# Decoder trunk on one core: merged columns written beside the last input tile, a second raw weight tile in the mixer, and its weights' low parts on GpSimd

## Chip, cores and metric

One NeuronCore of one Trainium2 chip runs the whole kernel in a single launch. The metric is the device time in microseconds. Two kernels are compared by the median of their runs.

## What is computed

The reference is one inference step of a decoder layer over 1024 prompt tokens and 8 sample tokens, in fp32. The stages are a half-step SwiGLU, a token mixer, cross-attention into 256 memory tokens and a second SwiGLU, each followed by a layer norm. The change lies in the mixer:

```python
def _mixer(h, S0, shift0, h0, buf0, P):
    proj = h @ P['w_in']                     # r, k, v, low-rank inputs, LRU input, GeLU gate, two merge gates
    ...
    S_new, y = _rwkv_scan(S0.astype(F32), rh, hd(decay), kh, vh, kk, hd(a))
    ...
    _, hs = lax.associative_scan(_lin_combine, (a_t, b_t), axis=1)
    lru_out = (hs * jax.nn.gelu(p_gelu.astype(F32))).astype(h.dtype)
    gates = jax.nn.sigmoid(p_gate).reshape(B, T, N_BRANCH, D_MODEL)
    merged = gates[:, :, 0] * rwkv_out + gates[:, :, 1] * lru_out
    out = merged @ P['w_mix_out']
    return out, S_new.astype(h.dtype), p_rwkv[:, -1], hs[:, -1].astype(h.dtype), new_buf
```

## The kernel before, in words

Activations lie with channels on the partitions: `HH` and `HL` hold the high and the low part (fp32 rounded for TensorE, and the rest) of 8 blocks of 128 channels by 1032 columns. Every product is three matmuls (`mm3`, L122 to L127): high by high, low by high, high by low. A weight block is made by `split_half` (L90): SP loads a raw tile of 128x512, ScalarE rounds it to `wh` (L99), VectorE subtracts to give `wl` (L100), and the raw tile is free again once both have read it.

The mixer's 16 heads are 8 pairs. After the low-rank inputs and the first two pairs' r, k, v, its long middle part has 16 units t (four pairs of pairs, `g`, by four pieces of 256 columns, `n`). A unit runs several generators side by side, recorded in 13 rounds (`rounds`, L49): `chain` of unit t-1 (the recurrence: each of four chunks has three products, with VectorE or ScalarE between them), `inverse` of unit t (31 dependent pairs of VectorE instructions, L548 and L930), `stage_unit` of t+1, `branches` (the LRU), `samples_b` or `samples_c` for the sample tokens, `post` of a finished chain, and a share of the filler. Each engine then runs its instructions in the order in which the recording and the framework's scheduler leave them; SP's queue carries every DMA of the kernel.

The filler is `gemms` (L658): 50 input tiles (`project`, L632), each 3 column groups of 344 by 8 blocks, then the 8 tiles of the output product over the first six blocks (`out_proj`, L1211). One step is two blocks, that is six matmuls; `FILL[t]` (L536) is the number of steps that unit t takes, and the last unit takes what is left. `load` is called behind each of a tile's first two groups and makes one half of the next tile's weight. There is one raw tile in this part (`S.rawseq`, L768) and four pairs of `wh`, `wl` (L769).

Merged blocks 0 to 5 go through DRAM (`MG`). The last input tile has to be done with a column group of `HH` before merged columns can take that group's place. In `out_proj`, at m == 0, each group waits for its six blocks: load `ev` from `MG`, ScalarE writes `HH`, VectorE writes `HL` (`direct`, L1031), one filler step for each block, and the group's matmuls follow:

```python
for m in range(KT):
    for c0, n in CH3:
        for k in range(kt) if m == 0 else ():
            ...
            e = tmp("ev", 344, 2)[:, :n]
            nc.sync.dma_start(out=e, in_=MG[k, :, c0:c0 + n])
            direct(k, c0, n, e)
            yield
        q = psg(n)
        yield from cols(W[m], c0, n, q, kt)
```

`ev` is also the tile through which every group's result leaves (L641, L1231). GpSimd's instructions in this part are the powers of `inv_norm` (L782, tiles `ivs` and `ivc`), a copy into `BN` (L875) and the powers for the sample tokens (L1126, L1197).

Of the kernel before, what the change touches and what calls it, by code (L numbers as in the profile page):

```python
# [10 lines left out]
F32 = mybir.dt.float32  # L11
# [8 lines left out]
NT = NP + NS  # L20
# [69 lines left out]
def split_half(S, src, nm="w", hp=None, view=lambda t: t, to=None):  # L90

    nc = S.nc
    raw = raw_tile(S)[:, :512]
    S.wdma.dma_start(out=view(raw), in_=src)
    if to is None:
        hp = hp or next(S.hlseq)
        to = [hp.tile([128, 512], F32R, tag=nm + x, name=nm + x) for x in "hl"]
    hi, lo = to
    nc.scalar.activation(out=hi, in_=raw, func=AF.Identity)  # L99
    nc.vector.tensor_tensor(out=lo, in0=raw, in1=hi.bitcast(F32), op=ALU.subtract)  # L100
    return hi, lo


# [371 lines left out]
def setup(ctx, tc, I):  # L475
    nc = tc.nc
    S = SimpleNamespace(tc=tc, nc=nc, pend=[])
    S.const = ctx.enter_context(tc.tile_pool(name="const", bufs=1))
    S.hp = ctx.enter_context(tc.tile_pool(name="hp", bufs=1))
    S.wraw = ctx.enter_context(tc.tile_pool(name="wraw", bufs=1))  # L480
    S.whl = ctx.enter_context(tc.tile_pool(name="whl", bufs=3))
    S.wdma = nc.sync
    S.dram = ctx.enter_context(tc.tile_pool(name="dram", bufs=1, space=bass.MemoryType.DRAM))
    S.ones_d = S.const.tile([128, 128], F32, name="ones_d")
    nc.vector.memset(S.ones_d, 1.0 / D)
    S.lng = S.const.tile([128, 4, KT], F32, name="lng")
    S.lnb = S.const.tile([128, 4, KT], F32, name="lnb")
    nc.sync.dma_start(out=S.lng, in_=I["ln_g"])
    nc.sync.dma_start(out=S.lnb, in_=I["ln_b"])
    S.mhalf = S.const.tile([128, 8], F32, name="mhalf")  # L490
    nc.vector.memset(S.mhalf, -0.5)
    S.ident = S.const.tile([128, 128], F32, name="ident")
    nc.sync.dma_start(out=S.ident, in_=I["cst"][:, 0:128])
    S.HH = S.hp.tile([128, KT, NT], F32R, name="HH")
    S.HL = S.hp.tile([128, KT, NT], F32R, name="HL")
    return S
# [36 lines left out]
DRAM = bass.MemoryType.DRAM  # L533
GR, GK, GV, GZ, GA, GL, GE, G1, G0, GG, GB, GM = range(12)

FILL = [42] * 11 + [37] * 5  # L536

LATE = ("ev", "ref", "dend", "scl", "sm", "wsb", "sf", "ysb", "gsq", "ivc", "lm")

# [1 line left out]
def mixer(octx, S, I, O, MG, HD, pre):  # L541
# [13 lines left out]
    with ExitStack() as ctx:  # L555
# [76 lines left out]
        def project(p, mt, gi, func, sc, w, cs, psg, pool, then=None):  # L632

            for c0, n in cs:
                q = psg(n)
                yield from cols(w, c0, n, q)
                if then and c0 < CH3[2][0]:
                    then()
                e = pool.tile([128, 344], F32, tag="ev", name="ev", bufs=2)[:, :n]
                ACT(e, q, func, scale=sc)  # L640
                nc.sync.dma_start(out=GD[p][:, gi, c0:c0 + n], in_=e)  # L641

# [15 lines left out]
        def gemms():  # L658
# [9 lines left out]
            W = [[] for _ in src]  # L668
            queue = itertools.chain(((W[j], x[:, 512 * i:512 * i + 512]) for j, x in enumerate(src) for i in range(2)))

            def load():
                for to, x in itertools.islice(queue, 1):
                    to.append(split_half(S, x))

            load()
            load()
            for j, (p, x, i) in enumerate(todo):
                yield from project(p, *x, W[j], CH3, psg, t1, load)
                ready.add((p, x[1]))
                if i in (2, 5):  # L680
                    ends(p, i == 2)
            ready.add("h")
            yield from out_proj(W[len(todo):], load)


        with ExitStack() as c2:
# [78 lines left out]
        actx = ctx.enter_context(ExitStack())  # L765
        stages = itertools.cycle([(st0, 1)] + [(actx.enter_context(tc.tile_pool(name="msa", bufs=4)), 2)] * 2)
        ta = actx.enter_context(tc.tile_pool(name="ma", bufs=1))
        S.rawseq = itertools.cycle([S.wraw])  # L768
        S.hlseq = itertools.cycle([S.whl] * 3 + [actx.enter_context(tc.tile_pool(name="mwhl", bufs=1))])  # L769
        pools.update(dict.fromkeys(("i", "m", "sc"), actx.enter_context(tc.tile_pool(name="mpa", bufs=1, space=PSUM))))  # L770

# [21 lines left out]
        def stage(U, i):  # L793
# [45 lines left out]
            yield  # L839
            pb = psm(w)  # L840
            nc.tensor.matmul(pb, ones1, s2, start=True, stop=True)
            bv = tmp("bv", 256, 2)
            TTo(bv, xv[:, 0:256], pb[:, 0:256], ALU.mult)
            nc.sync.dma_start(out=GD[p][:, GB, c0:c0 + 256], in_=bv)
            if n == 3:
# [124 lines left out]
        def branch(p, n, P):  # L970
# [36 lines left out]
            ACT(th, th, AF.Sqrt)  # L1007
            yield
            STT(gi, gi, 0.5, th, ALU.mult, ALU.mult)
            hs = tmp("lm", 264, 2)  # L1010
            nc.vector.tensor_tensor_scan(out=hs[:, 0:256], data0=gr[:, 0:256], data1=gi[:, 0:256],
                                         initial=0.0 if n == 0 else P.hl, op0=ALU.mult, op1=ALU.add)
            yield
# [194 lines left out]
            else:  # L1208
                direct(p, NP, NS, y)

        def out_proj(W, load):  # L1211

            kt = KT - 2
            for m in range(KT):
                for c0, n in CH3:
                    for k in range(kt) if m == 0 else ():
                        while not all(("mg", k, j) in ready for j in range(5) if c0 < (NT if j == 4 else 256 * j + 256) and
                                      256 * j < c0 + n):
                            yield

                        e = tmp("ev", 344, 2)[:, :n]
                        nc.sync.dma_start(out=e, in_=MG[k, :, c0:c0 + n])
                        direct(k, c0, n, e)
                        yield
                    q = psg(n)
                    yield from cols(W[m], c0, n, q, kt)
                    if c0 < CH3[2][0]:
                        load()
                    e = tmp("ev", 344, 2)[:, :n]
                    ACT(e, q, scale=1.0 / ALPHA)  # L1230
                    nc.sync.dma_start(out=FD[m, :, c0:c0 + n], in_=e)  # L1231

# [88 lines left out]
        actx.close()  # L1321
        S.norms = Norms(S, octx)
        more_weights(S, ctx, 2, 1)
        wp = ctx.enter_context(tc.tile_pool(name="wmix", bufs=4))
        fp = ctx.enter_context(tc.tile_pool(name="fmix", bufs=2))
        w = [[split_half(S, I["w_mix"][4 * i:4 * i + 4, :, 128 * k:128 * k + 128].rearrange("m p c -> p m c"), hp=wp,
# [383 lines left out]
```

## Time and profile before

| | before |
|---|---|
| median of 3 runs | 3221.41 us (3218.6 to 3223.76) |
| the profiled execution, its own time | 3223.72 us |
| its span from first to last instruction | 3221.9 us |
| mean granted TensorE clock | 0.964 |
| TensorE busy (PE) | 3029.4 us, 94% of the span |
| weight loads (PEld) | 2855.4 us, 89% |
| VectorE (DVE) busy | 2199.8 us, 68% |
| ScalarE (ACT) busy | 1433.5 us, 44% |
| GpSimd (POOL) busy | 560.8 us, 17% |

A busy share is an average over stages. A granted clock of 1 stands for 2.4 GHz and 0.5 for 1.2 GHz; a stretch in which both occurred shows a value between. Matmuls overlap, so the time of one in a dense run is the distance between two starts and not its own length. Line numbers are those of the kernel before.

### The profile page before, as it was taken

The page shows a single profiled execution, that of the slowest core. Times are in us where ns is not written, and L with a number is a line of the kernel's source. Part 1 is how long each engine was busy: PE and PEld are TensorE (multiplying, and loading weights), DVE is VectorE, ACT ScalarE, POOL GpSimd, SP SyncE. Part 2 cuts the span into 40 slices and gives each one's busy share as a digit, 9 for nine tenths or more (in the row PEclk, how much of TensorE's full clock was granted, in tenths as well). Part 3 has the DMA queues.
Part 4 walks back from the last instruction along what each step waited for, and adds up shares of the span by engine and source line. Part 5 has one row for each costly group of instructions (what it writes and reads, how often), then busy time and mean ns, then how long its engine had stood idle before and what let it go on. Part 6 is the DMA issues. An engine that isn't in the chain of part 4 may idle for free. (4 is left out here: it accounts for less than half of the span.)

```text
span 3221.9 us, 63123 instructions
## 1 busy us (share of the span) xinstructions
PE 3029.4 (94%) x23324; PEld 2855.4 (89%) x23324; DVE 2199.8 (68%) x5895; ACT 1433.5 (44%) x3192; POOL 560.8 (17%) x526
## 2 busy tenths in 40 slices
PE   8999999999999999998999888889898999999997
PEld 8999999999888888887888767688887999999997
DVE  7666665574357788777777777676677666666556
ACT  5333352125555565555555554464235433334112
POOL 2222200132000101010110100261005322220111
PEclk9999999999999999999999969799999999999998
DMA  4222253314544455445445544664433222225321
GB/s 140 80 79 80 80 162 106 106 54 145 192 117 127 135 142 147 118 135 147 141 126 140 144 140 115 200 186 133 148 121 116 79 80 80 80 80 157 107 86 53
DMA packets 381445, 386.72 MB, mean 120 GB/s; under 512 B 144048, under 2 KB 282320, under 8 KB 381136
## 3 DMA queue, kind: packets, MB, share of 16 engines
q1 hardware_dynamic: 381136, 382.69, 39.8%
q8 instruction: 183, 3.00, 0.4%
q14 instruction: 126, 1.03, 0.1%
HBM read 277.54 MB, written 105.23 MB: 119 GB/s over the span
## 5 line engine op out<-in xcount | busy, mean ns | idle before, releaser
L125 PE MATMUL ps<-HH,wh 128*128 128x258 f32 (+1 forms) x2384 | 718.3, 302 | 17.0 <-ACT HH L508 7.9
L126 PE MATMUL ps<-HL,wh 128*128 128x258 f32 (+1 forms) x2384 | 716.6, 301 | 0.0
L127 PE MATMUL ps<-HH,wl 128*128 128x258 f32 (+1 forms) x2384 | 715.7, 300 | 0.0
L125 PE MATMUL g<-HH,wh 128*128 128x344 f32 (+2 forms) x1840 | 625.0, 340 | 31.5 <-ACT wh L99 20.3
L127 PE MATMUL g<-HH,wl 128*128 128x344 f32 (+2 forms) x1840 | 598.9, 327 | 6.5 <-DVE wl L100 6.5
L126 PE MATMUL g<-HL,wh 128*128 128x344 f32 (+2 forms) x1840 | 602.0, 328 | 1.8 <-DVE HL L548 1.4
L125 PEld LDWEIGHTS ps<-HH,wh 128*128 128x128 f32 x2384 | 451.4, 189 | 19.2 <-ACT HH L508 7.9
L126 PEld LDWEIGHTS ps<-HL,wh 128*128 128x128 f32 x2384 | 450.9, 189 | 0.4 <-DVE HL L509 0.3
L127 PEld LDWEIGHTS ps<-HH,wl 128*128 128x128 f32 x2384 | 450.3, 189 | 0.0
L125 PEld LDWEIGHTS g<-HH,wh 128*128 128x128 f32 x1840 | 359.8, 196 | 50.3 <-ACT wh L99 22.6
L127 PEld LDWEIGHTS g<-HH,wl 128*128 128x128 f32 x1840 | 359.3, 196 | 12.2 <-DVE wl L100 8.0
L126 PEld LDWEIGHTS g<-HL,wh 128*128 128x128 f32 x1840 | 360.2, 196 | 9.3 <-DVE HL L548 3.4
L228 ACT ACTIVATE wh<-raw 128x512 fp32r<-128x512 f32 x280 | 176.4, 631 | 321.9 <-PE ps L126 264.8
L334 POOL TENSOR_TENSOR raw<-raw 128x512 f32<-128x512 f32 x160 | 214.1, 1338 | 566.2 <-DVE wl L229 351.3
L229 DVE TENSOR_TENSOR wl<-raw,wh 128x512 fp32r<-128x512 f32 x280 | 202.2, 723 | 138.9 <-ACT wh L228 132.0
L100 DVE TENSOR_TENSOR wl<-raw,wh 128x512 fp32r<-128x512 f32 x302 | 217.4, 726 | 109.9 <-ACT wh L99 104.8
L99 ACT ACTIVATE wh<-raw 128x512 fp32r<-128x512 f32 x302 | 185.5, 626 | 235.0 <-PE ps L126 78.0
L442 DVE SCALAR_TENSOR_TENSOR acc<-ps,acc 128x344 f32<-128x344 f32 x336 | 168.8, 512 | 144.2 <-PE ps L127 143.5
L548 DVE TENSOR_TENSOR pr<-tq,iv 128x2 f32<-128x2 f32 (+30 forms) x496 | 160.3, 323 | 2.9
L553 ACT ACTIVATE ev<-g 128x344 f32<-128x344 f32 x192 | 87.3, 455 | 127.9 <-PE g L127 97.5
L930 DVE TENSOR_REDUCE tq<-pr 128x1 f32<-128x2 f32 (+30 forms) x496 | 121.6, 245 | 2.8
L374 ACT ACTIVATE g<-g 128x258 f32<-128x258 f32 x160 | 67.1, 419 | 113.2 <-DVE g L333 113.2
(410 smaller groups left out, 6363.6 us busy)
## 6 DMA issues: line engine op xcount, KB each, us to landing
raw<-in_wi_dram SPq DMA_DIRECT2D x176, 256.0 KB
raw<-in_w_in_dram SPq DMA_DIRECT2D x116, 256.0 KB
GD<-ev SPq DMA_DIRECT2D x168, 172.0 KB
raw<-in_wo_dram SPq DMA_DIRECT2D x104, 256.0 KB
raw<-HID SPq DMA_DIRECT2D x88, 258.0 KB
HID<-g SPq DMA_DIRECT2D x80, 258.0 KB
tg<-GD SPq DMA_DIRECT2D x32, 512.0 KB
wt<-T SPq DMA_DIRECT2D x160, 64.0 KB
```

The costliest lines, as they stand in the source:

```text
L99: nc.scalar.activation(out=hi, in_=raw, func=AF.Identity)
L100: nc.vector.tensor_tensor(out=lo, in0=raw, in1=hi.bitcast(F32), op=ALU.subtract)
L125: nc.tensor.matmul(ps, wh, xh, start=first, stop=False)
L126: nc.tensor.matmul(ps, wh, xl, start=False, stop=False)
L127: nc.tensor.matmul(ps, wl, xh, start=False, stop=last)
L228: nc.scalar.activation(out=hi, in_=x, func=AF.Identity)
L229: nc.vector.tensor_tensor(out=lo, in0=x, in1=hi.bitcast(F32), op=ALU.subtract)
L334: pool_tt = lambda o, a, b, op: nc.gpsimd.tensor_tensor(out=o, in0=a, in1=b, op=op)
L442: nc.vector.scalar_tensor_tensor(out=a, in0=q, scalar=0.5 / ALPHA, in1=a, op0=ALU.mult, op1=ALU.add)
L548: TTo = lambda o, a, b, op: nc.vector.tensor_tensor(out=o, in0=a, in1=b, op=op)
L553: ACT = lambda o, a, f=AF.Identity, **kw: nc.scalar.activation(out=o, in_=a, func=f, **kw)
L930: nc.vector.tensor_reduce(out=tq[:, 0:m, i], in_=pv, axis=mybir.AxisListType.X, op=ALU.add)
```

## The change

Four things change in the mixer's middle part.

1. The merged columns of a group are no longer loaded and split at the head of `out_proj`. A generator `merged` for each group starts when the last input tile's matmuls of that group are recorded, and moves by two blocks at every following step of that tile. The last group's merges stay in `out_proj`, three steps instead of six.
2. The raw weight tile gets a second buffer (`mraw`), and `ev` a third. For their space `bv` and `lm` go from two buffers to one.
3. `FILL` goes from 37 to 34 steps in units 11 to 13 and to 40 in units 14 and 15.
4. `wl` of the weights made in this part, 116 of them, is subtracted by GpSimd in place of VectorE. Behind the units VectorE does it again.

```diff
-    nc.vector.tensor_tensor(out=lo, in0=raw, in1=hi.bitcast(F32), op=ALU.subtract)
+    S.low.tensor_tensor(out=lo, in0=raw, in1=hi.bitcast(F32), op=ALU.subtract)
...
-FILL = [42] * 11 + [37] * 5
+FILL = [42] * 11 + [34] * 3 + [40] * 2
...
-                if then and c0 < CH3[2][0]:
-                    then()
-                e = pool.tile([128, 344], F32, tag="ev", name="ev", bufs=2)[:, :n]
+                if then:
+                    then(c0, n)
+                e = pool.tile([128, 344], F32, tag="ev", name="ev", bufs=3 if then else 2)[:, :n]
...
-            for j, (p, x, i) in enumerate(todo):
+            for j, (p, x, i) in enumerate(todo[:-1]):
                 yield from project(p, *x, W[j], CH3, psg, t1, load)
...
-            ready.add("h")
-            yield from out_proj(W[len(todo):], load)
+            p, x, i = todo[-1]
+            merges = []
+            def then(c0, n):
+                load(c0, n)
+                merges.append(merged(c0, n))
+            for _ in project(p, *x, W[len(todo) - 1], CH3, psg, t1, then):
+                for m in merges:
+                    next(m, 0)
+                yield
+            ready.update(((p, x[1]), "h"))
+            yield from out_proj(W[len(todo):], load, merges)
...
-        S.rawseq = itertools.cycle([S.wraw])
+        S.rawseq = itertools.cycle([S.wraw, actx.enter_context(tc.tile_pool(name="mraw", bufs=1))])
+        S.low = nc.gpsimd
...
-            bv = tmp("bv", 256, 2)
+            bv = tmp("bv", 256)
...
-            hs = tmp("lm", 264, 2)
+            hs = tmp("lm", 264)
...
+        def merged(c0, n):
+            for k in range(KT - 2):
+                while not all(("mg", k, j) in ready for j in range(5) if c0 < (NT if j == 4 else 256 * j + 256) and
+                              256 * j < c0 + n):
+                    yield
+                e = tmp("ev", 344, 3)[:, :n]
+                nc.sync.dma_start(out=e, in_=MG[k, :, c0:c0 + n])
+                direct(k, c0, n, e)
+                if k % 2:
+                    yield
...
-                for c0, n in CH3:
-                    for k in range(kt) if m == 0 else ():
...
+                for j, (c0, n) in enumerate(CH3):
+                    if m == 0:
+                        yield from merges[j]
...
+        S.low = nc.vector
```

SP's queue in unit 13, where the merges begin. `GD7<-ev` is the result of one of the last input tile's column groups on its way out, `ev<-MG` the load of one merged block, `raw` a half of an output weight, and the rest belongs to the units. Before:

```order
L641 DMA GD7_8811<-ev_23177 128x344
L1222 DMA ev_23180<-MG_81 128x344
L1222 DMA ev_23184<-MG_81 128x344
L1185 DMA e0_25225<-GD7_8811 128x8
L1222 DMA ev_23188<-MG_81 128x344
L1060 DMA MG_81<-ysb_22842 128x256
L1043 DMA tg_23346<-GD6_8810 128x4x256
L1222 DMA ev_23221<-MG_81 128x344
L844 DMA GD7_8811<-bv_23205 128x256
L1222 DMA ev_23225<-MG_81 128x344
```

Now:

```order
L643 DMA GD7_8811<-ev_23118 128x344
L1233 DMA ev_23128<-MG_81 128x344
L1233 DMA ev_23132<-MG_81 128x344
L94 DMA raw_23400<-in_w_mix_dram 128x512
L1233 DMA ev_23142<-MG_81 128x344
L94 DMA raw_23483<-in_w_mix_dram 128x512
L1200 DMA e0_25210<-GD6_8810 128x8
L1233 DMA ev_23146<-MG_81 128x344
L1233 DMA ev_23156<-MG_81 128x344
L1075 DMA MG_81<-ysb_22789 128x256
L643 DMA GD7_8811<-ev_23205 128x344
```

Before, the row at the top is the tile's third group and no group's result follows among the merges; now it is the first, the second (last row shown, five rows left out ahead of it) leaves after the first group's merges, and two halves of output weights are loaded among them.

GpSimd's queue in the same kind of unit, some units earlier: `ivs` and `ivc` are the powers that a stage and a finished chain wait for, `BN` the copy in a stage. Before:

```order
L875 COPY BN_19192<-BN_19192 64x4x64
L782 TENSOR_TENSOR ivc_19327<-ivc_19327,mhalf_75 128x4
L1197 TENSOR_TENSOR w8_19292<-w8_19292,mhalf_75 128x8
L782 TENSOR_TENSOR ivs_19499<-ivs_19499,mhalf_75 128x4
L875 COPY BN_19617<-BN_19617 64x4x64
L782 TENSOR_TENSOR ivc_19888<-ivc_19888,mhalf_75 128x4
```

Now:

```order
L100 TENSOR_TENSOR wl_19385<-raw_19382,wh_19384 128x512
L1212 TENSOR_TENSOR w8_19295<-w8_19295,mhalf_75 128x8
L100 TENSOR_TENSOR wl_19541<-raw_19538,wh_19540 128x512
L100 TENSOR_TENSOR wl_19630<-raw_19627,wh_19629 128x512
L797 TENSOR_TENSOR ivs_19502<-ivs_19502,mhalf_75 128x4
L890 COPY BN_19620<-BN_19620 64x4x64
L100 TENSOR_TENSOR wl_19787<-raw_19784,wh_19786 128x512
L100 TENSOR_TENSOR wl_19876<-raw_19873,wh_19875 128x512
L797 TENSOR_TENSOR ivc_19891<-ivc_19891,mhalf_75 128x4
```

One or two low parts now stand ahead of nearly every power and copy.

TensorE's program tells how the filler is spread. Between the ends of two units' inverses it holds this many filler matmuls:

| unit | 7 | 8 | 9 | 10 | 11 | 12 | 13 | 14 | 15 |
|---|---|---|---|---|---|---|---|---|---|
| before | 252 | 228 | 276 | 252 | 231 | 221 | 166 | 168 | 246 |
| now | 252 | 252 | 252 | 252 | 212 | 212 | 194 | 216 | 198 |

The table counts rows of the program. In the same program the chain's twelve products (three for each of four chunks) are spread unevenly at the end: in unit 13, now, the last nine stand with 24 filler matmuls among them and the rest of the filler behind, where before the first nine had 60 among them and the last three came 72 later; in unit 14, now, eleven stand with 18 among them, where before they were spread over 150.

## Rows read from the trace of the kernel before

**Rows 1.** The page, busy time of each engine over the span, with its share and its instructions.

```profile
PE 3029.4 (94%) x23324; PEld 2855.4 (89%) x23324; DVE 2199.8 (68%) x5895; ACT 1433.5 (44%) x3192; POOL 560.8 (17%) x526
```

**Rows 2.** Windows from the start of one unit's inverse (the memset of its tile `iv`) to the next, units 7 to 15 in order; the last ends where the filler ends. Columns: the stretch and its length in us, busy time of PE, PEld, DVE, ACT and POOL with instructions, granted clock, share of the DMA engines, GB/s.

```profile
1389.40:1462.60 73.20, 68.89 (x589) 60.47 (x588) 58.16 (x189) 41.95 (x91) 6.37 (x6) 0.98 0.53 142
1462.60:1540.80 78.20, 70.17 (x563) 62.30 (x562) 58.15 (x197) 42.02 (x94) 5.57 (x6) 0.91 0.52 146
1540.80:1607.20 66.40, 64.15 (x568) 56.79 (x567) 50.76 (x183) 40.34 (x96) 9.27 (x8) 1.00 0.48 139
1607.20:1676.20 69.00, 66.16 (x577) 59.24 (x576) 52.41 (x194) 39.15 (x94) 9.20 (x8) 0.98 0.46 126
1676.20:1748.50 72.30, 70.11 (x596) 60.42 (x595) 56.33 (x185) 40.51 (x89) 5.62 (x6) 0.98 0.55 147
1748.50:1827.70 79.20, 70.45 (x566) 59.57 (x566) 58.61 (x202) 41.12 (x92) 5.17 (x6) 0.89 0.51 135
1827.70:1898.90 71.20, 58.71 (x434) 46.11 (x433) 59.93 (x210) 43.44 (x106) 9.89 (x9) 0.76 0.44 124
1898.90:1972.30 73.40, 66.23 (x471) 56.06 (x470) 49.44 (x173) 42.95 (x100) 7.68 (x6) 0.86 0.46 134
1972.30:2041.20 68.90, 52.10 (x385) 44.99 (x384) 51.29 (x175) 27.76 (x53) 2.20 (x2) 0.85 0.50 130
```

**Rows 3.** Timeline of SP in units 13 and 15: start, duration (with what merged rows span), queue, line, DMA.

```profile
1878.81 9.42 SPq L1222 DMA_DIRECT2D ev<-MG  x2
...
2021.85 0.55 SPq L1174 DMA_DIRECT2D out_srwkv_dram<-ws  x1
2022.49 0.38 SPq L94 DMA_DIRECT2D raw<-in_w_mix_dram  x1
```

**Rows 4.** Windows of 5 us in unit 13, columns as in rows 2.

```profile
1865.00:1870.00 5.00, 4.01 (x23) 3.10 (x24) 4.96 (x21) 3.27 (x9) 0.78 (x1) 0.50 0.30 59
1885.00:1890.00 5.00, 4.21 (x36) 2.98 (x35) 4.01 (x15) 2.09 (x6) 1.12 (x1) 0.50 0.20 61
```

**Rows 5.** Timeline of PE in unit 15, two filler matmuls at the high clock and two at the low one: start, duration, line, operation.

```profile
2012.33 0.32 PE L127 MATMUL g<-HH,wl 128*128 128x344 f32 x1
2012.49 0.32 PE L125 MATMUL g<-HH,wh 128*128 128x344 f32 x1
...
2028.39 0.49 PE L127 MATMUL g<-HH,wl 128*128 128x344 f32 x1
2028.67 0.49 PE L125 MATMUL g<-HH,wh 128*128 128x344 f32 x1
```

**Rows 6.** Who PE waited for in the units, 880 to 2040 us: total, times, longest.

```profile
PE g L125 <- ACT wh L99: 19.0, 7, 6.7
PE m L788 <- ACT s L553: 16.2, 11, 5.0
...
PE g L127 <- DVE wl L100: 6.5, 3, 3.3
```

**Rows 7.** Timeline of PE, stalls on weights; in brackets the idle time ahead of the instruction and what ended it.

```profile
1184.61 0.66 PE L125 MATMUL g<-HH,wh 128*128 128x344 f32 x1 [3.55 <-ACT wh L99]
...
1471.40 0.66 PE L125 MATMUL g<-HH,wh 128*128 128x344 f32 x1 [4.18 <-ACT wh L99]
...
2003.17 0.66 PE L127 MATMUL g<-HH,wl 128*128 128x344 f32 x1 [2.75 <-DVE wl L100]
...
2026.64 0.66 PE L125 MATMUL g<-HH,wh 128*128 128x344 f32 x1 [6.66 <-ACT wh L99]
```

**Rows 8.** Timeline of ACT around two of these stalls.

```profile
1183.32 0.42 ACT L553 ACTIVATE cs<-cs 128x256 f32<-128x256 f32 x1 [0.66 <-DVE tq L930]
...
1183.95 0.61 ACT L99 ACTIVATE wh<-raw 128x512 fp32r<-128x512 f32 x1
...
2003.35 0.46 ACT L553 ACTIVATE ev<-g 128x344 f32<-128x344 f32 x1 [4.42 <-DMA FD<-ev]
...
2025.96 0.63 ACT L99 ACTIVATE wh<-raw 128x512 fp32r<-128x512 f32 x1 [2.75 <-DMA raw<-in_w_mix_dram]
```

**Rows 9.** Who SP's queue waited for at the raw weight loads (L94) in the units: total, times, longest.

```profile
SPq L94 <- DVE tq L930: 36.9, 21, 5.3
...
SPq L94 <- DVE pr L548: 21.1, 17, 3.2
```

**Rows 10.** Groups by line in the units, 880 to 2040 us: VectorE's largest group (the products in the inverse), its low parts, and GpSimd's powers of the stages. Columns: count, busy time and mean ns of one, idle time ahead of them and what ended it.

```profile
L548 DVE TENSOR_TENSOR pr<-tq,iv 128x2 f32<-128x2 f32 (+30 forms) x496 | 160.3, 323 | 2.9
...
L100 DVE TENSOR_TENSOR wl<-raw,wh 128x512 fp32r<-128x512 f32 x110 | 75.4, 686 | 33.0 <-ACT wh L99 31.4 <-DMA R<-GD 0.8 <-PE sc L881 0.5
L782 POOL TENSOR_TENSOR ivs<-ivs,mhalf 128x4 f32<-128x4 f32 x31 | 33.4, 1076 | 273.3 <-DVE ivs L551 235.7 <-DVE iv L922 25.2 <-ACT QZ L553 12.0
```

**Rows 11.** By tile over the whole span: GpSimd's sums of raw weights in the SwiGLU stages, and VectorE's low parts of merged blocks; duration min/median/max in ns.

```profile
L334 POOL TENSOR_TENSOR raw<-raw x160: 1270/1296/2296, 34.9 to 2901.0; 128x512 f32<-128x512 f32 x160
L548 DVE TENSOR_TENSOR HL<-ev,HH x18: 498/510/519, 1857.9 to 1924.2; 128x344 fp32r<-128x344 f32 x18
```

**Rows 12.** Timeline of the first SwiGLU, GpSimd and VectorE side by side.

```profile
113.25 2.95 POOL L334 TENSOR_TENSOR raw<-raw 128x512 f32<-128x512 f32 x2 [7.90 <-DVE u L333]
...
114.16 0.42 DVE L333 TENSOR_TENSOR u<-u,ps 128x258 f32<-128x258 f32 x1 [0.54 <-PE ps L127]
...
114.97 1.78 DVE L229 TENSOR_TENSOR wl<-raw,wh 128x512 fp32r<-128x512 f32 x1
```

More of the change, by code (lines that the diff above doesn't have):

```diff
@@ L669, in gemms, with load @@
             queue = itertools.chain(((W[j], x[:, 512 * i:512 * i + 512]) for j, x in enumerate(src) for i in range(2)))
-            def load():
-                for to, x in itertools.islice(queue, 1):
+            def load(c0=0, n=0):
+                for to, x in itertools.islice(queue, c0 < CH3[2][0]):
                     to.append(split_half(S, x))
@@ L1209, in samples_c, with out_proj @@
                 direct(p, NP, NS, y)
-        def out_proj(W, load):
-            kt = KT - 2
-            for m in range(KT):
-                for c0, n in CH3:
-                    for k in range(kt) if m == 0 else ():
[L1217 to L1224, printed above, removed]
+        def merged(c0, n):
[8 more added lines that the diff above has]
+                    yield
+        def out_proj(W, load, merges):
+            for m in range(KT):
+                for j, (c0, n) in enumerate(CH3):
+                    if m == 0:
+                        yield from merges[j]
                     q = psg(n)
[L1226 to L1229, printed above, removed]
+                    yield from cols(W[m], c0, n, q, KT - 2)
+                    load(c0, n)
+                    e = tmp("ev", 344, 3)[:, :n]
                     ACT(e, q, scale=1.0 / ALPHA)
@@ L1323, in mixer @@
         more_weights(S, ctx, 2, 1)
+        S.low = nc.vector
         wp = ctx.enter_context(tc.tile_pool(name="wmix", bufs=4))
```

## Prediction

> **What bounds the kernel now.** I read the page's busy times first: PE is busy for 94% of the span, DVE for 68% [rows 1]. So TensorE's work is nearly the time, and what can be won is its idle time and the time that it spends at the lower of its two clocks. The second view is the windows by unit of the mixer's middle part [rows 2]. The reader is to compare units at the same place of their four: 13 with 9, 14 with 10, 15 with 7, 12 with 8. Unit 9 takes 66.4 us, with PE busy for 64.15 at a granted clock of 1.00, and its program holds 276 filler matmuls. Unit 13 has 166 of them and still takes 71.2 us, with 12.5 us of idle PE and a clock of 0.76. Units 14 and 15 stand at 0.86 and 0.85. The third view is the timelines of unit 13: one pair of merge loads stands 9.42 us at SP's head [rows 3], and in two 5 us windows among the merges the clock is 0.50, that is 1.2 GHz [rows 4]. What TensorE did there was little: filler was not allowed yet, since it waits for the merged columns. At the low clock a filler matmul starts every 0.28 us, at the high one every 0.16 [rows 5]; 0.158 is the value that I use below for the high clock, the mean of a dense run. The fourth view is the waits of PE: weights cost it 19.0 + 6.5 = 25.5 us [rows 6], of which the stalls of 6.66 and 2.75 us lie in unit 15 [rows 7].
>
> The sum is made against the profiled execution, 3223.7 us, which is 2.3 us above the median of the runs, 3221.4.
>
> **Part 1, the merges beside the last input tile, with the new steps (units 13 and 14).** The work is unchanged: 18 loads, 18 ScalarE roundings and 18 VectorE subtractions of 510 ns [rows 11]. What moves is the order: the first and second group's merges run while PE still has the tile's other groups. So unit 13 gets 28 more filler matmuls (166 to 194) and unit 14 gets 48 more (168 to 216), which is 76 x 0.158 = 12.0 us of PE work taken into idle time. If PE were the only limit, both units would fall to their models: 71.2 - 66.4 = 4.8 and 73.4 - 69.0 = 4.4 us [rows 2]. DVE does not allow all of it: it is busy for 59.9 of 71.2 us in unit 13, against 50.8 in unit 9, and the chain's products now stand close together in TensorE's program, where every one waits for VectorE or ScalarE. I take -4 for unit 13 and -2 for unit 14. Bounds: the idle time and the half-clock time of both units, 12.5 + 7.2 + 0.24 x 71.2 + 0.14 x 73.4 = 47 us of gain, and a loss of 12 us if the moved matmuls all came on top. I stay by the model units, the nearest rows.
>
> **Part 2, fewer steps elsewhere.** Unit 15 has 48 filler matmuls fewer: 48 x 0.158 = 7.6 us. There the filler runs to the end, and DVE is busy for only 51.3 of 68.9 us [rows 2], so most of it counts: -6. The third `ev` buffer helps in the same place, where ScalarE waited 4.42 us for the tile's last store [rows 8]. Bounds: 0 and -16 (the 7.6, and the stalls of 2.75 and 6.66). Units 11 and 12 have 28 fewer: at most 4.4 us. But unit 12 took 79.2 us with 221 where unit 8 took 78.2 with 228, so steps do not set the time of that unit; I take -2, between 0 and -4.4.
>
> **Part 3, the second raw tile.** SP waited 36.9 + 21.1 = 58 us for VectorE at the raw loads [rows 9], and every DMA behind waited too. That wait goes; the next one at SP's head, a group's result that waits for PE, takes part of its place. Outside unit 15 the weights cost PE about 15 us. Two of these stalls, 3.55 and 4.18 us, are not cured by an earlier load: at 1183.95 ScalarE had its raw tile and was held by VectorE through the instruction ahead [rows 7, 8]; nor is the one at 2026.64, whose load stood at SP behind a store of the sample state [rows 3, 8]. That leaves 7 us in reach. A lower clock follows a stall, as in units 8 and 12 at 0.91 and 0.89 [rows 2], so I take -5; bounds 0 and -20. The program shows what helps here: units 8 and 9 now hold 252 each in place of 228 and 276.
>
> The buffers given up cost nothing. `bv` and `lm` are written twice a unit, so some 32 us apart, and their stores have that long; if SP ever lagged by a half unit, VectorE would stand for the rest of the store.
>
> **Part 4, low parts on GpSimd.** VectorE gives up 116 subtractions of 0.686 us, 80 us, and 31.4 us in which it stood in front of them waiting for ScalarE [rows 10]. GpSimd takes 116 of about 1.30 us, the time of its sums of the same shape [rows 11]. It has room: it stood 273.3 us in front of the stages' powers alone. But it is not free for others. At 114.97 a VectorE subtraction took 1.78 us, where it takes about 0.69 alone, beside a GpSimd instruction of the same shape [rows 12, 10]; 0.42 us operations that read PSUM, as at 114.16, were not longer. So a low part on GpSimd can hold VectorE for nothing or for 1.30 us. VectorE's largest group in the units, 160.3 us [rows 10], reads both operands from SBUF, others read PSUM, and the engine is idle for a quarter of the time; so I take half of 1.30, 0.65, against the 0.69 given up: net zero. A power that finds a low part ahead of it in GpSimd's queue comes up to 1.3 us later, 60 powers, at most 78 us of latency; PE already waits 16.2 us for ScalarE's instructions behind them [rows 6]. In the other direction stand the 31.4 us. I take 0, bounds -10 and +20.
>
> The Trainium skill (SBUF — State Buffer, Who interferes with whom) states that a VectorE instruction with two SBUF inputs contends with a GpSimd instruction that reads SBUF, and that the second to start is blocked until the first ends. The row agrees: 1.78 us is the rest of the GpSimd row and then somewhat less than a free subtraction [rows 12]. By that rule a low part that always met such an instruction would cost the full 1.30 us; this is the first rival.
>
> **Sum:** -4 - 2 - 6 - 2 - 5 + 0 = -19 us: 3204.7 in a profiled execution, 3202.4 as a median. The part behind the units is only moved forward.
>
> **The rivals.**
> *GpSimd's low parts hold VectorE (slower).* Each costs VectorE 1.30 - 0.69 = 0.61 us net, 116 of them 71 us. VectorE is busy for 75% of a unit [rows 2], so some of it falls into its idle time; the mechanism decides from the point at which more than 19 of the 71 us reach PE. If half does, with the gains above: +35 - 19 = +16, 3237. For it: rows 12, and the stalls at 1184.61 and 1471.40, which come through a VectorE that has no gap. Against it: the 31.4 us of waits that VectorE loses. Chance 0.12.
> *The end is not set by where the merges stand.* Units 13 and 14 stay where they are, since VectorE is nearly full in 13 and the chain is bunched in 14: parts 1 and 3 give nothing, unit 15 gives 4 and units 11 and 12 give 2: -6, 3215.4. For it: 84% of DVE in unit 13. Against it: PE's 12.5 idle us at half clock in the same unit. Chance 0.18.
> *The dips go too.* If weights never stop PE, the clock stays at 2.4 GHz in units 7 to 12. Its loss there is the missing share by each length: 1.5 + 7.0 + 0 + 1.4 + 1.4 + 8.7 = 20 us [rows 2]. Then -39: 3182.4. For it: the even filler of units 8 and 9. Against it: dips also follow waits for the powers [rows 6]. Chance 0.15.
>
> **The numbers.** My forecast, 3202.4, has 0.55; its own range is 3191 to 3214. A measurement tells 0.2%, 6.4 us, from no change. Faster (below 3215.0): 0.53 of the forecast, the 0.15 of the dips and 0.04 of the second rival, 0.72. Slower: the first rival, 0.12. The rest, 0.16, is no difference. The range goes from 3181 to 3227: it takes in the dips' case, the second rival and the lower end of the first, up to a net loss of 6 us; outside lie most of the first rival and the parts' gains beyond the dips' case.
>
> **What would show it.** Right: unit 13 near 67 us and unit 15 near 63, with clocks above 0.85; no wait of SP's L94 for a low part; `wl` at some 1.3 us on GpSimd; filler of units 13 and 14 starting without a stall on `HH`. Wrong: VectorE's busy time in the units not falling by some 40 us or more, its two-operand instructions longer (the first rival); units 13 and 14 at 71 to 73 us with a low clock (the second); PE waiting for `wl` on GpSimd, or more for ScalarE's instruction behind a power, which would mean that the queue on GpSimd is the cost.

## The result and the profile after

The changed kernel takes **3267.9 us** (median of 4 runs, 3263.2 to 3277.2) against 3222.1 us (3218.6 to 3223.8) of the kernel before on the same chip: ratio 1.0141, 95% interval 1.0122 to 1.0159. It is slower by 46 us. The forecast was 3202.4, in a range of 3181 to 3227: wrong in sign, and outside its range.

The page of the changed kernel, busy time of each engine over the span (3270.2 us):

```profile
PE 3034.2 (93%) x23324; PEld 2859.3 (87%) x23324; DVE 2209.1 (68%) x5779; ACT 1428.9 (44%) x3190; POOL 718.0 (22%) x642
```

Against [rows 1], VectorE ran 116 instructions fewer, and yet it was busy for 9.3 us more, so its other instructions grew. The growth is about 74 us: the changed kernel's busy time less that of e10 below, which makes no low parts at all. (It is less than 9.3 + 116 x 0.686 = 89 us, since VectorE's instructions overlap in the trace: those of the kernel before add up to 2510 us in 2199.8 us of busy time.) PE's busy time rose by 4.8 us only; the rest of the loss is PE's idle time.

Windows by unit, of the changed kernel: units 7, 8, 12, 13, and 15 as far as its filler goes; columns as in [rows 2].

```profile
1397.20:1479.70 82.50, 74.61 (x650) 66.98 (x648) 57.13 (x177) 40.49 (x91) 17.56 (x14) 0.94 0.49 137
1479.70:1562.90 83.20, 75.51 (x608) 65.00 (x605) 63.02 (x203) 48.22 (x104) 16.10 (x14) 0.94 0.50 141
...
1777.50:1857.90 80.40, 70.72 (x590) 57.68 (x588) 59.60 (x199) 38.73 (x89) 12.25 (x11) 0.87 0.48 130
1857.90:1946.00 88.10, 70.52 (x488) 58.29 (x486) 61.58 (x194) 44.78 (x108) 20.05 (x16) 0.77 0.45 130
...
2011.50:2075.00 63.50, 45.98 (x362) 37.35 (x360) 49.60 (x164) 28.46 (x53) 7.92 (x7) 0.86 0.44 117
```

Unit 13, forecast at 67 us with a clock above 0.85, takes 88.1 us with 17.6 us of idle PE at 0.77. Unit 15 is near the forecast 63. What the forecast did not have is in VectorE's groups. Groups by line of the changed kernel in the units (880 to 2085 us), the inverse's products, a convolution of the LRU, and the low parts, now on GpSimd; columns as in [rows 10]:

```profile
L550 DVE TENSOR_TENSOR pr<-tq,iv 128x2 f32<-128x2 f32 (+30 forms) x496 | 192.1, 387 | 4.1 <-DVE iv L937 0.3
...
L100 POOL TENSOR_TENSOR wl<-raw,wh 128x512 fp32r<-128x512 f32 x110 | 150.5, 1372 | 432.2 <-ACT wh L99 407.8 <-PE ch L1096 8.7 <-PE g L127 6.1
...
L551 DVE SCALAR_TENSOR_TENSOR xc<-cb,vec,xc 128x256 f32<-128x256 f32 x93 | 54.3, 584 | 7.3 <-ACT xc L555 7.1
```

The products `pr` grew from 160.3 us to 192.1 with the same 496 instructions. The timeline of the changed kernel shows one such growth; GpSimd's rows first, then VectorE's (start, duration, line, operation):

```profile
933.32 1.28 POOL L100 TENSOR_TENSOR wl<-raw,wh 128x512 fp32r<-128x512 f32 x1 [10.29 <-ACT wh L99]
...
933.49 1.30 DVE L550 TENSOR_TENSOR pr<-tq,iv 128x100 f32<-128x100 f32 x1
934.83 0.26 DVE L945 TENSOR_REDUCE tq<-pr 128x5 f32<-128x100 f32 x1
```

A product of 100 columns, 0.17 us behind the start of a low part, lasts until 0.19 us after its end; the one of 95 columns just before it takes 0.33 us. A second place of the same trace has both kinds of neighbour:

```profile
1314.63 1.27 POOL L100 TENSOR_TENSOR wl<-raw,wh 128x512 fp32r<-128x512 f32 x1 [3.17 <-DMA TT<-D]
...
1314.81 0.59 DVE L550 TENSOR_TENSOR QZ<-ch,scl 64x128 f32<-64x128 f32 x2 [0.38 <-PE ch L1112]
1315.43 1.02 DVE L1026 TENSOR_TENSOR_SCAN lm<-gr,gi 128x256 f32<-128x256 f32 x1
```

The two `QZ` instructions read PSUM and one SBUF tile and take 0.295 us each beside the low part, their usual mean being 0.286. The scan reads two SBUF tiles and takes 1.02 us, where the eight scans of this form in the units of before take 0.68 in the mean. The Trainium skill (SBUF — State Buffer, Who interferes with whom) draws the line there, between one and two SBUF inputs, and the trace agrees beside the low parts. Beside GpSimd's small powers it does not; the last section has the numbers.

Waits of the changed kernel in the same stretch: total, times, longest, for PE, ACT, GpSimd and SP.

```profile
PE m L803 <- ACT s L555: 29.7, 12, 7.4
PE m L1013 <- DVE xc L551: 17.9, 4, 14.5
PE sc L911 <- DVE SC L550: 16.0, 19, 1.9
...
PE g L127 <- POOL wl L100: 1.4, 3, 0.5
PE g L125 <- ACT wh L99: 1.1, 2, 0.7
```

```profile
ACT s L555 <- POOL ivs L797: 69.3, 31, 11.0
...
POOL wl L100 <- ACT wh L99: 407.8, 84, 19.1
...
SPq L94 <- POOL wl L100: 57.1, 34, 4.6
```

PE's stalls on weights, 25.5 us in [rows 6], are 2.5 us now. In their place it waits for VectorE and for what comes from it: `s` 29.7 against 16.2, `SC` 16.0, `xc` 17.9. How little of that is the mark of the low parts on GpSimd, e10 shows below. SP's wait at the raw loads is nearly what it was, 57.1 against the 58 of [rows 9], now for GpSimd. ScalarE's 69.3 us for `ivs` left a rival cause open: GpSimd standing at a low part, for `wh`, with a power behind it.

### The profile page after: what moved, and what is told of

Same layout as the page of the kernel before. It is cut to its first block, busy times and chain, and to the rows that moved or that the text cites. A ratio compares the mean times of both kernels' runs of the same rounds, so it can differ in the third digit from the quotient of the medians.

```text
span 3270.2 us, 63270 instructions
## 1 busy us (share of the span) xinstructions
PE 3034.2 (93%) x23324; PEld 2859.3 (87%) x23324; DVE 2209.1 (68%) x5779; ACT 1428.9 (44%) x3190; POOL 718.0 (22%) x642
## 5 line engine op out<-in xcount | busy, mean ns | idle before, releaser
L229 DVE TENSOR_TENSOR wl<-raw,wh 128x512 fp32r<-128x512 f32 x280 | 204.3, 730 | 138.9 <-ACT wh L228 132.0
L100 POOL TENSOR_TENSOR wl<-raw,wh 128x512 fp32r<-128x512 f32 x116 | 158.3, 1368 | 481.5 <-ACT wh L99 457.0
L550 DVE TENSOR_TENSOR pr<-tq,iv 128x2 f32<-128x2 f32 (+30 forms) x496 | 192.1, 387 | 4.1 <-DVE iv L937 0.3
L100 DVE TENSOR_TENSOR wl<-raw,wh 128x512 fp32r<-128x512 f32 x186 | 139.3, 760 | 73.7 <-ACT wh L99 72.1
L464 POOL TENSOR_TENSOR acc<-acc,raw 128x516 f32<-128x516 f32 x32 | 42.8, 1341 | 418.7 <-DVE acc L442 415.2
```

Source lines behind the costliest of these rows:

```text
L100: S.low.tensor_tensor(out=lo, in0=raw, in1=hi.bitcast(F32), op=ALU.subtract)
L229: nc.vector.tensor_tensor(out=lo, in0=x, in1=hi.bitcast(F32), op=ALU.subtract)
L464: nc.gpsimd.tensor_tensor(out=a, in0=a, in1=x, op=ALU.add)
L550: TTo = lambda o, a, b, op: nc.vector.tensor_tensor(out=o, in0=a, in1=b, op=op)
```

## The experiments

Differences are in medians against the kernel before on the same chip; intervals are those of the ratio.

**One part alone.** Four kernels: the changed one with the low parts back on VectorE; before with the low parts on GpSimd only; before with the second raw tile only (`bv` and `lm` single); the changed one with one raw tile and the low parts on VectorE, so the merges, the third `ev` and the new steps.

```diff
 e1_no_pool (from the changed kernel)
-        S.low = nc.gpsimd
+        S.low = nc.vector
 e2_pool_only (from before; lows on VectorE again behind the units)
-    nc.vector.tensor_tensor(out=lo, in0=raw, ...
+    S.low.tensor_tensor(out=lo, in0=raw, ...
+        S.low = nc.gpsimd
 e3_raw_only (from before)
-        S.rawseq = itertools.cycle([S.wraw])
+        S.rawseq = itertools.cycle([S.wraw, actx.enter_context(tc.tile_pool(name="mraw", bufs=1))])
 e4_merges_only (from the changed kernel)
-        S.rawseq = itertools.cycle([S.wraw, actx.enter_context(tc.tile_pool(name="mraw", bufs=1))])
-        S.low = nc.gpsimd
+        S.rawseq = itertools.cycle([S.wraw])
+        S.low = nc.vector
```

> The change with the low parts of the mixer's weights back on VectorE; merges, second raw tile and steps stay. If the low parts on GpSimd are the cost: 3200 us, about 20 below the kernel before, as the other parts were forecast, unit 13 near 67 us. If the bunched end (the chain's products without filler among them) is the cost: 3260 or more, unit 13 still near 88 us. If both: about 3235.

> The kernel before with its mixer's low parts on GpSimd and nothing else; one raw tile. If the low parts on GpSimd are the cost: 3270 to 3290 us (45 and the 20 that the other parts would have brought), with SP's raw loads waiting for GpSimd's low parts and ScalarE's instructions behind the powers late. If the bunched end is the cost: 3222 within 6.

> The kernel before with the second raw tile (and one buffer each for bv and lm, for its space), nothing else. If its worth is as forecast: 3217 us, SP's waits at raw loads near zero. If the single buffers of bv or lm cost, above 3228, with VectorE waiting for their stores.

> The merges beside the last input tile with the new steps and the third ev buffer; one raw tile, low parts on VectorE. If the forecast of these parts holds: 3208 us, units 13 to 15 shorter by 12 us together. If the bunched end costs: above 3228, with unit 13 above 80 us.

Measured: e1 3212.0 us, -10.5 (0.9961, 0.9948 to 0.9973); e2 3290.7, +68.2 (1.0208, 1.0187 to 1.0228); e3 3225.1, +2.6 (1.0004, 0.9993 to 1.0015); e4 3225.5, +3.0 (1.0008, 0.9997 to 1.0019). The loss is the low parts on GpSimd, +56 by taking them out and +68 by adding them. The other parts win 10.5 us together and nothing apart. Half of the 20 us that I had expected of e1 came; e3 and e4 show nothing of the 5 and 14 that I had expected of them; e2 is at the top of its range.

**Work or wait.** Three kernels from before, whose low parts stay on VectorE. Each adds 116 GpSimd instructions where the low parts stand in GpSimd's queue. In the traces PE, VectorE, ScalarE and SP run the same instructions in the same order as before, but for two memsets of `iv` that change place with a neighbour in e5 and e9 and a few rows of PE and ScalarE in e9. So a new order is hardly the cause of a difference, as it could be in e2. For the room of the scratch tile, e5 and e9 have one buffer each for `bv` and `lm`, as the changed kernel has and e6 has not; no wait of VectorE in their units ends at a store of either, and e3 has the single buffers and costs nothing. A NoSync edge gives an instruction its place in a queue without a wait.

```diff
+        def side(hi, a):
 e6_queue_only: a wait for wh, nearly no work
+            x = nc.gpsimd.tensor_tensor(out=sc, in0=hi[:, 0:4].bitcast(F32), in1=hi[:, 4:8].bitcast(F32), ...
 e5_port_only: 128x512, no wait; a NoSync edge to wh's rounding sets its place
+            x = nc.gpsimd.tensor_tensor(out=sc, in0=sc, in1=sc, ...
 e9_port_and_queue: 128x512, behind wh
+            x = nc.gpsimd.tensor_tensor(out=sc, in0=hi.bitcast(F32), in1=hi.bitcast(F32), ...
```

> The kernel before, low parts on VectorE as there, plus behind each rounded weight of the units a tiny GpSimd instruction (128 x 4, two slices of the rounded weight into a scratch tile that nothing reads): 116 of them, at the places of GpSimd's queue where the low parts would stand. The orders of TensorE, VectorE, ScalarE and SP are those of before, row for row. It puts the wait for ScalarE's rounding at GpSimd's head and nearly no work. Theory 1 (the wait at the head of GpSimd's queue holds the powers behind it): +20 to +45 us, 3242 to 3267, ScalarE's wait for ivs (48.6 us in the units of before) at 60 to 75. Theory 2 (GpSimd's reading and writing of SBUF slows VectorE): within 5 us of before. Theory 3 (the framework's scheduler puts the whole program in another order when the low parts change engine): within 5 us.

> The kernel before, low parts on VectorE as there, plus 116 GpSimd subtractions of the low parts' shape (128 x 512) from a scratch tile to itself, at the same places of GpSimd's queue, which wait for nothing but GpSimd; the tiles bv and lm get one buffer each in place of two, for room. The orders of the other engines are those of before. It is the work without the wait: the SBUF traffic beside VectorE, and up to 1.3 us for a power that comes behind. Theory 1: +5 to +20, 3227 to 3242. Theory 2: +45 to +75, since VectorE keeps its own 80 us of low parts: 3267 to 3297, with VectorE's pr at 380 ns or more against 323. Theory 3: 0 to +15.

> As the kernel before with 116 GpSimd subtractions of 128 x 512 that read the rounded weight and write a scratch tile: the wait at GpSimd's head and the work, with the low parts still made by VectorE and the orders of the other engines those of before. Theory 1: +40 to +65, 3262 to 3287, more than the two parts alone. Theory 2: +45 to +80, as with the work alone. Theory 3: +5 to +20, since most of the +68 us of the kernel before with its low parts on GpSimd would be the new order.

Measured: e6 3220.2, -0.4 (1.0003, 0.9993 to 1.0014); e5 3277.9, +57.3 (1.0178, 1.0164 to 1.0192); e9 3261.8, +41.2 (1.0133, 1.0115 to 1.0150). Theory 1 falls. GpSimd's and ScalarE's waits of e6 in the units:

```profile
POOL sc L776 <- ACT wh L99: 575.9, 96, 18.4
...
ACT s L556 <- POOL ivs L792: 49.3, 26, 7.3
```

GpSimd stands 575.9 us at its head for `wh`, and ScalarE's wait for `ivs` stays at 49.3 us (48.6 before). Its wait for the other power, `ivc`, does grow, from 27.7 us to 42.8, and the end does not move. What costs is the 128x512 work beside VectorE. That work also stands in front of a power, which is a rival of its own, but ScalarE's wait for `ivs` is 51.8 us in e5 and for `ivc` 28.1, so ScalarE hardly waited longer for a power there, and the kernel lost 57 us. From the pages of e5 and then of e9, the engines' busy times and the group of the inverse's products (160.3 us, 323 ns in [rows 10]):

```profile
PE 3052.2 (93%) x23324; PEld 2872.0 (88%) x23324; DVE 2249.8 (69%) x5895; ACT 1435.9 (44%) x3192; POOL 692.9 (21%) x643
...
L551 DVE TENSOR_TENSOR pr<-tq,iv 128x2 f32<-128x2 f32 (+30 forms) x496 | 176.8, 356 | 2.9
```

```profile
PE 3041.6 (93%) x23324; PEld 2862.4 (88%) x23324; DVE 2258.0 (69%) x5895; ACT 1434.6 (44%) x3192; POOL 720.7 (22%) x643
...
L551 DVE TENSOR_TENSOR pr<-tq,iv 128x2 f32<-128x2 f32 (+30 forms) x496 | 181.9, 367 | 2.9
```

The same 5895 instructions keep VectorE busy for 50.0 and 58.2 us more, 0.43 and 0.50 us for each GpSimd instruction, and the kernels take 57 and 41 us longer. In e9, where 66 of the low parts on VectorE themselves run beside a GpSimd instruction, a part of the growth is theirs, which may fall on time that VectorE has; that this is why e9 is cheaper than e5 was not shown. My 380 ns for `pr` was too high, the time was within what I gave to the traffic in e5 and 4 us below it in e9.

**What VectorE's own low parts cost.** From e1, no low parts in the units on any engine; the third product of a filler group multiplies a constant tile.

```diff
 e10_no_low
-        S.low = nc.vector
+        S.low = None
+        S.zero = ... .tile([128, 512], F32R, name="zero")
```

> The changed kernel with no low parts in the units at all, on no engine: the third product of each filler group multiplies a constant tile instead (part of the computation is left out). Beside the same kernel with the low parts on VectorE (3212.0) it measures what VectorE's 80 us of low parts cost the end, and beside the changed kernel (3267.9) what GpSimd's cost. Theory A (the low parts lay in VectorE's idle time, so that giving them up is worth little, and all of the loss is the hold on VectorE's chain): 3200 to 3212. Theory B (half of VectorE's time reaches the end, as the forecast assumed): 3165 to 3180, and the hold then costs some 90 us, more than the 81 us that VectorE's instructions grew. Theory C (the order that the scheduler finds once the low parts have left VectorE is the bad thing): 3230 or more.

Measured: 3188.3, -32.5 (0.9905, 0.9887 to 0.9924). The page of e10:

```profile
PE 2998.3 (94%) x23324; PEld 2834.0 (89%) x23324; DVE 2135.4 (67%) x5779; ACT 1426.7 (45%) x3190; POOL 559.8 (18%) x526
```

It lies between theories A and B, and tells both prices. Low parts on VectorE (e1) cost the end 32.5 - 10.5 = 22 us, where VectorE is busy for 2199.5 - 2135.4 = 64 us more: 0.34 us for a microsecond. Low parts on GpSimd (the changed kernel) cost 45.8 + 32.5 = 78 us, where the same instructions on VectorE are 2209.1 - 2135.4 = 74 us longer: 1.06 for a microsecond. Theory C falls for e10's order, an order without low parts on VectorE; but the three kernels' orders are not the same, so both prices hold some of that, too.

In the profiled executions the changed kernel's span is 84 us above e10's: 48 us of it are PE's idle time and 36 its busy time. The second is the clock: PE is busy at the lower level, 0.5, for 201.9 us in the changed kernel and for 136.8 in e10 (summed from the traces' clock records), and 65 us of work at half speed take 33 us more than at full speed. Single waits do not show the hold: e10, which has none and is the fastest kernel here, has PE waiting 24.0 us for `s`, 18.4 for `xc` and 11.2 for `SC`, against 29.7, 17.9 and 16.0.

Open stays why e2 (+68) is dearer than e9 (+41), where VectorE makes the low parts as well: in e2 PE waits 16.7 us for `wh` and 9.7 us for GpSimd's `wl`, and its order is a new one; the two were not told apart.

**The steps.** The old steps with the changed kernel's other parts, three ways; then one step less in the first eleven units.

```diff
 e8_old_steps (from e1), e11_merges_old_steps (from e4), e12_after_old_steps (from the changed kernel)
-FILL = [42] * 11 + [34] * 3 + [40] * 2
+FILL = [42] * 11 + [37] * 5
 e13_steps_41 (from e8)
-FILL = [42] * 11 + [37] * 5
+FILL = [41] * 11 + [37] * 5
```

> The changed kernel with its low parts on VectorE (3212.0 us, 10.5 below before) and the old steps of filler (37 in the last five units in place of 34, 34, 34, 40, 40). If the steps carry the 10.5 us, as the forecast's terms for units 11, 12 and 15 had it (-8 of -19): 3218 to 3223. If the merges beside the input tile and the second raw tile carry it together: 3208 to 3215. If it comes from the order that the scheduler happens to find: anywhere between 3205 and 3225, and no unit moves as its steps do.

> Part 1 of the forecast by itself: the merges beside the last input tile and the third ev buffer, one raw tile, low parts on VectorE, and the old steps (37 in the last five units). With the new steps it took 3225.5, as before. If the new steps cost some 9 us here too, as they did beside the second raw tile (3212.0 against 3203.1): 3213 to 3219, and the forecast's -6 for the merges holds. If the gain needs the second raw tile: 3220 to 3226.

> The changed kernel, low parts on GpSimd, with the old steps. If the steps cost the same whatever engine makes the low parts: 3256 to 3262. If the new steps fit a VectorE that is held by GpSimd: 3265 to 3275.

> The fastest version so far (3203.1: merges beside the last input tile, second raw tile, low parts on VectorE, old steps) with 41 steps of filler in place of 42 in the first eleven units: eleven steps, some 11 us of TensorE's work, go to the last unit. There TensorE stands 14.0 us for one xc of VectorE, since the filler is used up and the last two pieces of the LRU, which share one buffer by way of DRAM, lie bare. If that bare chain is what takes back part of the gain, the filler fills it: the stall falls below 6 us and the time to 3191 to 3200. If the first units are set by their own chains and not by their steps, they stay as long, and the last unit only gets longer: 3203 to 3214.

Measured: e8 **3203.1**, -17.5 (0.9947, 0.9934 to 0.9959); e11 3225.5, +4.7 (1.0018, 1.0007 to 1.0029); e12 3255.4, +34.6 (1.0111, 1.0092 to 1.0130); e13 3219.3, -0.9 (1.0002, 0.9991 to 1.0013). e8 beats both kernels and lies below every range that I had given; e11 is in the range of "needs the second raw tile", e12 just below its first one. The new steps cost 7 us beside the second raw tile (e1, e8), 11 with the low parts on GpSimd (the changed kernel, e12), and nothing without the second tile (e4, e11). With the old steps the merges give nothing alone (e11, whose interval lies a little above 1) and the second raw tile nothing alone (e3), and the two together 17.5 us. PE's waits for weights and for `xc` in the units, of e11, then of e8:

```profile
PE g L125 <- ACT wh L99: 18.0, 9, 4.9
PE m L1013 <- DVE xc L551: 17.0, 6, 14.4
```

```profile
PE m L1013 <- DVE xc L551: 16.0, 4, 14.0
...
PE g L125 <- ACT wh L99: 4.2, 2, 3.3
```

So PE waits 14 us less for rounded weights in e8. But that is not where the 22 us between e11 and e8 lie: by the pages PE is idle for 198.1 us in e11 and for 198.2 in e8, as other waits grew, and for 192.5 in the kernel before. What fell is PE's busy time, 3029.4 us before, 3024.3 in e11 and 2999.0 in e8, for the same 23324 matmuls, and of it the part at the lower clock: 179.7, 155.2 and 118.3 us. Against before, 61 us fewer at half speed save 31 us, and PE's busy time is 30.4 us less. So e8's gain is TensorE's clock and not idle time that was filled; which waits let the clock fall was not looked into.

The wait for `xc` is new in all kernels with the merges. It stands in unit 15, where the filler has run out. The timeline of e8 there, SP, ScalarE, VectorE and PE:

```profile
1997.94 0.43 SPq L1041 DMA_DIRECT2D GD<-lm  x1
...
1998.47 0.38 SPq L1000 DMA_DIRECT2D cb<-GD  x1
...
2000.80 0.61 ACT L555 ACTIVATE xc<-cb,vec 128x264 f32<-128x264 f32 x1 [8.31 <-DMA cb<-GD]
...
2002.51 0.48 DVE L551 SCALAR_TENSOR_TENSOR xc<-cb,vec,xc 128x256 f32<-128x256 f32 x1
...
2003.27 1.22 PE L1013 MATMUL m<-xc,wg 128*128 128x264 f32 x2 [14.02 <-DVE xc L551]
```

In SP's queue the next piece of the LRU is loaded only behind the store of the one before it, and PE has nothing else. In e13 the eleven steps that were saved for this place fill it:

```profile
2021.29 0.68 PE L1013 MATMUL m<-xc,wg 128*128 128x264 f32 x2 [2.86 <-DVE xc L551]
```

Yet e13 lost all of e8's gain. The first eleven units, as one window each, of e8 and of e13 (columns as in [rows 2]):

```profile
912.60:1651.60 739.00, 703.83 (x6105) 628.08 (x6103) 570.54 (x1968) 435.58 (x998) 72.67 (x73) 0.99 0.49 137
```

```profile
918.60:1666.10 747.50, 707.01 (x6037) 625.35 (x6036) 569.29 (x1965) 424.94 (x988) 77.94 (x73) 0.98 0.48 135
```

They take 8.5 us more with eleven steps fewer, so fewer steps did not make them shorter, and they begin 6.0 us later. Every such edit also gives the scheduler's order another form. The loss is larger than the 0 to 11 us that I had put down for this case. By the pages PE is idle for 9 us less than in e8 and busy for 25 us more. How much of e1's, e8's, e10's and e13's differences is the parts and how much the order is not separated here; for e5, e6 and e9, which have the order of before, the question hardly arises.

## Why the prediction was wrong

**Part 4, low parts on GpSimd: 0 forecast, -10 to +20 as bounds, +56 measured (e1 to the changed kernel).** This is the step that failed, at the sentence "so I take half of 1.30, 0.65, against the 0.69 given up: net zero". The mechanism was there and its size was right: VectorE's growth was 74 us, which is 0.64 us for each of 116 low parts. The 0.69 given up was too high, since it counts time in which the next instruction already runs: taking the low parts out saved 64 us of busy time (e1 to e10), 0.55 each. That makes a net of 10 us, and the kernel lost 56. So the netting was wrong. It set a microsecond that VectorE loses against a microsecond that it is given, as if both had the same price at the end. e10 gives the prices: 22 us for the low parts that VectorE makes and 78 us for the hold. In shape this is the first rival (chance 0.12), but the rival had the hold at 1.30 us and a half of the net reaching PE; here the hold is about half of that, and what it costs at the end, the clock included, is as much as all of it. Why the prices differ is shown only in part: 32 us of the growth lie in `pr`, one of two instructions that follow each other 31 times in an inverse, with 4.1 us of idle VectorE in front of 496 of them, and 9.8 in `xc`; for VectorE's low parts PE waits only 2.9 us in all in e1. An inverse, from its first product to its last, takes 35.7 us in the mean in e10 and 38.9 in the changed kernel, 51 us more for the sixteen, beside 78 at the end; from before to e5 it grows from 35.8 to 37.8, 32 us of 57. So much of the loss can stand in the inverses, but not all of it, and that they are the chain that sets a unit is argued, not shown by a run of its own.

**The queue on GpSimd.** The "at most 78 us of latency" for the powers cost nothing (e6). The sign that I had named for it, more of PE's wait for ScalarE's instruction behind a power, did appear (29.7 against 16.2), and it pointed to the wrong cause: e10, with no low part on GpSimd, has 24.0 of it.

**Part 3, the second raw tile: -5 forecast.** The waits of PE for weights went as forecast, in the changed kernel even to 2.5 us. Alone the tile gave nothing (e3): in e3 they fell too, from 25.5 to 13.9 us, the time did not. SP's wait at the raw loads, of which I wrote "That wait goes", did not go: for the same two instructions of VectorE it is 28.0 us in e3 and 44.3 in e1, and with the low parts on GpSimd it came back as a wait for GpSimd, 57.1 us.

**Part 1, the merges: -6 forecast.** Alone nothing (e11), with the second raw tile 17.5 us for both (e8), where the two terms and no change of steps made -11. The forecast had no tie between the two; the merges' loads and the weights stand in one queue of SP, and e11 has the weight waits that e8 has not. Nor did the gain come as forecast. I had it as "PE work taken into idle time", in units 13 and 14; e8's PE is as idle as before and faster in its busy time. Units 13 and 14 take 73.6 and 67.1 us in e8 against 71.2 and 73.4; with the new steps, as the forecast had them, they take 78.1 and 76.4 (e1).

**Part 2, the steps: -8 forecast, +7 and +11 measured.** The wait for `xc` in unit 15 is not what they cost: it is there with the old steps too (12.1 us in e1, 16.0 in e8). Windows of units 12 to 14 of e1 and then of e8, columns as in [rows 2]:

```profile
1723.20:1805.40 82.20, 69.88 (x568) 57.58 (x568) 55.80 (x195) 36.74 (x82) 4.34 (x5) 0.90 0.49 133
1805.40:1883.50 78.10, 67.44 (x526) 57.34 (x526) 60.79 (x209) 46.60 (x113) 11.71 (x10) 0.81 0.47 133
1883.50:1959.90 76.40, 70.97 (x470) 63.78 (x469) 51.52 (x177) 40.99 (x98) 8.79 (x6) 0.86 0.45 124
```

```profile
1725.80:1797.60 71.80, 63.37 (x508) 53.28 (x508) 54.94 (x190) 36.17 (x81) 4.42 (x5) 0.93 0.51 145
1797.60:1871.20 73.60, 58.72 (x476) 51.86 (x477) 60.61 (x207) 47.77 (x116) 10.09 (x9) 0.88 0.53 151
1871.20:1938.30 67.10, 63.95 (x560) 55.09 (x559) 51.90 (x185) 39.47 (x96) 8.61 (x7) 1.00 0.50 143
```

These three take 24 us more with the new steps. Unit 11 is 7 us shorter and what lies behind unit 14 is 9 us shorter, as forecast and more. So the forecast of what fewer steps win was about right there, and what it left out is that the rest of the middle part gets longer by more; whether by the steps or by the new order is not separated. e13 points the same way as the sentence "so steps do not set the time of that unit", said of unit 12.

With the low parts left on VectorE and the steps left alone the kernel is at 3203.1 us, beside a forecast of 3202.4 for the whole change. That is luck: two of the forecast's parts are not in that kernel, and the two that are there won by the clock and not by the idle time that the terms had counted.

## What to carry to other kernels

Before work moves to GpSimd, list VectorE's instructions that read two SBUF tiles and stand in a dependent chain: each can be held for the rest of a large GpSimd instruction beside it (128x512 here). What VectorE is relieved of was worth a third of its time here; that it pays only as far as it was on that chain is how I read it, not shown. A busy microsecond has no one price; 64 us cost 22 here and 74 us cost 78. To tell a wait in a queue from traffic, add the wait and the work apart, on scratch data, so that the other queues keep their order.

## What the hardware showed

GpSimd's being busy is not what holds VectorE. In the trace of before, 189 VectorE instructions run beside GpSimd's 62 powers `ivs` and `ivc` (128 x 4, 1.07 us each); against the medians of their groups, shape by shape, they are not longer at all (-0.4 us together), though 48 of them are `pr`, `xc`, `AR`, `BN` or `s`, which are held beside low parts. In the changed kernel 294 run beside 110 low parts (128 x 512, 1.37 us) and are 71.9 us longer. Nor are the 266 longer that run beside the 128 x 4 subtractions of e6 (0.52 us each, 0.1 us in all). So in these two sizes it goes by how much GpSimd reads and writes, and not by its being busy. ScalarE's instructions are not longer: on the page of e5 it is busy for 1435.9 us, against 1433.5. GpSimd's subtraction itself takes 1.16 us from one scratch tile (e5), 1.36 from a rounded weight (e9) and 1.37 as a low part.
